# The last norm's factor scaled into the rows of w_ff1 by ScalarE, and four low parts given to VectorE

## The chip, the cores and the metric

The kernel runs on one core of one Trainium2 chip. The metric is the device time of one execution in microseconds (us). PE is TensorE's matmul row, DVE is VectorE, ACT is ScalarE, POOL is GpSimd and SP is SyncE, which issues most of the DMAs.

## What is computed

A block of a streaming encoder over 1024 tokens of 1024 features, float32. First a mixer (convolution and RWKV-7), then cross-attention with four heads into 256 memory tokens, then the MLP. What matters here is the end of the reference:

```python
x = x + cross_attention(rmsnorm(x, g_cross[l]), rmsnorm(mem, g_mem[l]), wq[l], wk[l], wv[l], wo[l])
hf = rmsnorm(x, g_ffn[l])
x = x + jnp.square(jax.nn.relu(hf @ w_ff1[l])) @ w_ff2[l]
return rmsnorm(x, g_final)

def rmsnorm(x, g):
    y = x * lax.rsqrt(jnp.mean(x * x, axis=-1, keepdims=True) + RMS_EPS)
    return y * g
```

`g_ffn` has one factor for each of the 1024 features, which are the columns of the normed tokens and the rows of `w_ff1` (1024 x 4096).

## The kernel before

All matmuls are done in three passes on pairs of a rounded high part and a low part: `split` (L70) makes the high part by a cast on ACT (L72) and the low part by a subtraction (L73), on VectorE unless another engine is given. `mm3` (L75) issues the three matmuls (L81 to L83).

The program is written as a flow of tiles, and a planner orders the instructions of each engine at build time, by a simulated timeline and by priorities (those of the order of the text, unless `at` or `shifted` moves them). On the chip each engine runs its instructions in that order. Tiles of one tag take turns in the tag's buffers. PSUM tiles of the MLP and of the attention come from a ring of eight banks (`bank`, L65): mm, pr, ep, cp, mm, pr, py, us; each user takes the next.

The attention (`attention`, L1092) goes head by head. In the last head (h == 3) the values of row block i, 128 tokens, are multiplied and added to the residual `x1[i]` (L1154), `x1[i]` is stored to `dx` (L1178), and the block is normed: `rms_scale` (L230) takes squares on ACT with their sum (L235), a sum and scale on DVE (L90) and the power -0.5 on POOL (L95); then `norm` (L242) multiplies by the token's factor and by `g_ffn` in one instruction on DVE (L246). The broadcast `g` is loaded ahead of the values of head 2 (L1172).

The up product of the MLP is a Strassen scheme with seven products. `blocks` (L1203) forms the token operands: for row blocks 0 to 3 it transposes two halves on PE (L1214) and splits them; for row blocks 4 to 7 it first takes four differences (L1238, on POOL, for block 7 on DVE), and transposes and splits five operands. Row block i follows two blocks behind the values (`feed`).

The weight operands are made by `up_operands` (L1289) for each of 16 pairs, a pair being 256 columns of `w_ff1`: two loads of 128x4x256 (L1296) into buffers that take turns (`ms`, `ms`, `w`, `w`), sums on DVE, seven splits. The first two splits of pairs 0 and 1 are given a priority of their own, inside the attention (`early`). `up` (L1325) multiplies; while it works on pair p, the operands of pair p + 1 are made, one for each product.

Of the kernel before, what the change touches and what calls it, by code (L numbers as in the profile page):

```python
# [9 lines left out]
F32 = mybir.dt.float32  # L10
F32R = mybir.dt.float32r
AF = mybir.ActivationFunctionType
ALU = mybir.AluOpType
# [4 lines left out]
P = 128  # L18
S = 1024
D = 1024  # L20
KC = D // P
# [30 lines left out]
class Trunk:  # L52
# [189 lines left out]
    def norm(self, pool, src, g, own=False):  # L242

        t, r = self.rms_scale(pool, src)
        t = src if own else t
        self.nc.vector.scalar_tensor_tensor(t, src, r, g, ALU.mult, ALU.mult)  # L246
        return t

    def features(self, t, hi, lo):
# [23 lines left out]
    def run(self):  # L273
        tc, nc, a = self.tc, self.nc, self.a
# [3 lines left out]
        def push(stack, name, bufs=1):  # L278
            cm = self.pool(name, bufs=bufs, side="right" if stack is right else None, reuse_waits="tile")
            stack.append(cm)  # L280
            return cm.__enter__()
# [5 lines left out]
        with ctx:  # L287
# [46 lines left out]
            x1 = {i: px1.tile([P, D], F32, name=f"x1_{i}") for i in (0, 4, 1, 5, 2, 6, 3, 7)}  # L334
# [23 lines left out]
            self.outs = 8  # L358
            pop(left, 2)
            pn = push(left, "pn")  # L360
            self.skip(pn, 320)
            ph1 = push(left, "ph1")
            h1 = self.norm_tiles(ph1, "h1")
            pG = push(left, "pG")
            g = self.gain(pn, "g_cross")
# [157 lines left out]
    def mixer_in(self, pc, pb, px, pl, pW, pz, hT):  # L523
# [29 lines left out]

        self.identity(pc)
        t = norm(0)
        w = conv_weights(0)
        for i in range(4):
            features(t, i)
            if i < 3:
                t = norm(i + 1)  # L560
        self.constants(pc, px)
        ts = [norm(4), norm(5)]
        conv(0, 0, *w)
        self.tap(TE[0], TE[3])
# [527 lines left out]
    def attention(self, pT, pQ, pG, pn, h1, x1, ahead, swap):  # L1092
        nc, ps = self.nc, self.ps
        scale = 256.0 ** -0.5

        def queries(h, w0=None):

            w = [w0 or self.wq_in(pG, h, 0), self.wq_in(pG, h, 1)]
            q = []
            for e in range(2):  # L1100
                for f in range(2):
                    hi, lo = (pQ.tile([P, HALF], F32R, tag="q" + t, name="q" + t, bufs=4) for t in "hl")
                    self.split(hi, lo, self.project(w[f], h1, e, P))
                    q.append((hi, lo))
            return q

        def values_in(h):
            v = []
            for m in range(2):
                st = self.pm.tile([P, D], F32, tag="ms", name="vst", bufs=2)  # L1110
                nc.sync.dma_start(st, self.dv[h, m])
                hi, lo = (pT.tile([P, D], F32R, tag=f"v{t}{m}", name="v" + t) for t in "hl")
                self.split(hi, lo, st)
                v.append((hi, lo))
            return v

        def scores(q, k, j):

            pp = self.bank(ps, "mm").rearrange("p (e m) -> p e m", m=M)
            for e in range(2):  # L1120
                ts_ = slice((2 * j + e) % 4 * P, (2 * j + e) % 4 * P + P)
                self.mm3(pp[:, e, :], [tuple(z[:, ts_] for z in q[j // 2 * 2 + f]) for f in range(2)], k)
            mx = pT.tile([P, 2], F32, tag="mx", name="mx", bufs=4)
            nc.vector.tensor_reduce(mx, pp, AX.X, ALU.max)
            nc.vector.tensor_scalar(mx, mx, -scale, None, ALU.mult)
            pe = pT.tile([P, 2, M], F32, tag="pe", name="pe", bufs=4)
            sm = pT.tile([P, 2], F32, tag="sm", name="sm", bufs=4)
            for e in range(2):
                nc.scalar.activation(
                    pe[:, e, :], pp[:, e, :], AF.Exp, bias=mx[:, e : e + 1], scale=scale, accum_out=sm[:, e : e + 1],  # L1130
                )
            nc.vector.reciprocal(sm, sm)
            for e in range(2):
                nc.vector.tensor_scalar(pe[:, e, :], pe[:, e, :], sm[:, e : e + 1], None, ALU.mult)
            return pe

        def turn(pe):
            phi, plo = (self.py_tile(F32R).rearrange("p (m t) -> p m t", m=2) for _ in range(2))
            pp = self.bank(ps, "mm")
            for m in range(2):  # L1140
                for e in range(2):
                    nc.tensor.transpose(
                        pp[:, (2 * m + e) * P : (2 * m + e + 1) * P], pe[:, e, m * P : (m + 1) * P], self.ident
                    )
            self.split(phi, plo, pp.rearrange("p (m t) -> p m t", m=2))
            return phi, plo

        def values(p, v, i):
            ts_ = slice((i % 2) * P, (i % 2) * P + P)
            for n in range(2):  # L1150
                cs = slice(n * 512, n * 512 + 512)
                pp = self.bank(ps, "mm")
                self.mm3(pp, [tuple(z[:, m, ts_] for z in p) for m in range(2)], [tuple(z[:, cs] for z in v[m]) for m in range(2)])
                nc.vector.tensor_tensor(x1[i][:, cs], pp, x1[i][:, cs], ALU.add)  # L1154

        norms = []

        def feed():
            self.blocks(*norms.pop(0), x1, B)

        q = queries(0, ahead[0])
        pe = [scores(q, ahead[1], j) for j in range(4)]
        for h in range(4):
            v = values_in(h)
            if h < 3:
                q, k = queries(h + 1), self.keys_in(pG, h + 1)
            p = [turn(t) for t in pe]
            if h < 3:
                pe = [scores(q, k, j) for j in range(4)]
            if h == 2:  # L1170
                B = swap()
                g = self.gain(pn, "g_ffn")  # L1172
            for i in range(8):
                values(p[i // 2], v, i)
                if h == 3:
                    if i > 1:
                        feed()
                    nc.sync.dma_start(self.dx[i], x1[i])  # L1178
                    norms.append((i, self.norm(pn, x1[i], g, i < 4)))
                    if i == 2:  # L1180
                        early = [self.tc.cur_priority]
        return B, feed, early
# [106 lines left out]
    def up_operands(self, p, out):  # L1289

        nc = self.nc
        st = []
        for k in range(2):
            w = next(self.wring)()
            src = self.a["w_ff1"][0, k * 512 : k * 512 + 512, p * 256 : p * 256 + 256]
            nc.sync.dma_start(w, src.rearrange("(k p) n -> p k n", p=P))  # L1296
            st.append(w)
        (a11, a21), (a12, a22) = ((w[:, :, 0:P], w[:, :, P:]) for w in st)

        def put(j, src, eng=None):  # L1300
            z = next(self.sring)().rearrange("p e (k f) -> p e k f", f=P)
            self.split(z[:, 0], z[:, 1], src, eng)
            out[j] = z[:, 0], z[:, 1]

        def temp():
            return self.temp().rearrange("p (k f) -> p k f", f=P)

        put(1, a11, nc.gpsimd if p < 2 else None)
        yield
        put(2, a12, nc.gpsimd)  # L1310
        yield
        s1 = self.both(temp(), a21, a22, ALU.add)
        s2 = self.both(temp(), s1, a11, ALU.subtract)
        put(6, s2)
        yield
        put(7, self.both(temp(), a11, a21, ALU.subtract))
        yield
        put(5, s1, nc.gpsimd)
        yield
        put(3, self.both(s2, a12, s2, ALU.subtract))  # L1320
        yield
        put(4, a22, nc.gpsimd)
        yield
# [252 lines left out]
```

## Time and profile before

| | us |
|---|---|
| median of 3 runs | 1571.23 (1570.77 to 1571.47) |
| profiled execution | 1571.13 |
| its span, from first to last instruction | 1569.4 |
| PE busy in the span | 1497.8 (95%) |
| DVE busy | 1167.2 (74%) |
| ACT busy | 665.1 (42%) |
| POOL busy | 530.9 (34%) |

Busy times are means over stages with different limits. In the rows below a time is counted from the span's start; a row's tile names are the program's (out<-in), and the brackets behind a row name the idle time ahead of it and what ended it.

### The profile page before, as it was taken

The numbers are of one execution on the slowest core, as the hardware profiler recorded it, in microseconds if no ns is written. First come the engines' busy times: TensorE is split into PE (matmuls) and PEld (weight loads), VectorE is DVE, ScalarE is ACT, GpSimd is POOL, SyncE is SP. The second block draws the span as 40 slices with busy tenths as digits, with TensorE's granted clock in tenths as the row PEclk, the third lists the DMA queues.
The fourth block names the chain that finished last, engine by engine and source line by source line (L and its number), as shares of the span: only waits on it lengthen the run. The fifth ranks groups of instructions, "written<-read, shape, count | busy, mean of one in ns | idle before, by whom it ended". The sixth has DMA issues, their size and how long they took to land. (4 is left out here: it accounts for less than half of the span.)

```text
span 1569.4 us, 22056 instructions
## 1 busy us (share of the span) xinstructions
PE 1497.8 (95%) x8114; PEld 1222.8 (78%) x8114; DVE 1167.2 (74%) x1721; ACT 665.1 (42%) x1223; POOL 530.9 (34%) x436
## 2 busy tenths in 40 slices
PE   6999887899999999999999979999999899999998
PEld 4777765668877778888888858888888788888886
DVE  5989898997889988475443787766666388578995
ACT  4522323122456653354231345555555345444454
POOL 4212337432443532431110064544444321003362
PEclk9999998897999999999999989999999999999999
DMA  7134445337334523312110132444444496563323
GB/s 236 48 128 156 124 117 171 112 117 195 108 94 123 162 98 99 101 47 81 41 41 28 52 122 86 170 152 156 156 149 157 152 382 198 178 200 87 102 80 121
DMA packets 175725, 201.14 MB, mean 128 GB/s; under 512 B 12191, under 2 KB 116951, under 8 KB 175618
## 3 DMA queue, kind: packets, MB, share of 16 engines
q1 hardware_dynamic: 168706, 187.15, 38.1%
q10 hardware_dynamic: 6912, 12.59, 2.2%
q8 instruction: 64, 1.05, 0.3%
q14 instruction: 43, 0.35, 0.1%
HBM read 139.92 MB, written 59.77 MB: 127 GB/s over the span
## 5 line engine op out<-in xcount | busy, mean ns | idle before, releaser
L629 DVE SCALAR_TENSOR_TENSOR acc<-u,cw,acc 128x1024 f32<-128x1024 f32 (+1 forms) x150 | 204.5, 1363 | 3.8
L267 POOL TENSOR_TENSOR wlo<-wst,whi 128x1024 fp32r<-128x1024 f32 (+2 forms) x34 | 86.8, 2556 | 135.9 <-ACT whi L266 135.9
L1238 POOL TENSOR_TENSOR p<-p,p 128x512 f32<-128x512 f32 x32 | 60.8, 1931 | 196.6 <-DVE p L1497 173.0
L73 DVE TENSOR_TENSOR s<-f,s 128x512 fp32r<-128x512 f32 x48 | 53.7, 1123 | 53.3 <-ACT s L72 53.3
L1343 ACT ACTIVATE y<-y 128x512 f32<-128x512 f32 x64 | 40.5, 633 | 82.0 <-DVE y L1238 74.3
L457 PE MATMUL mm<-memT,wkv 128*128 128x256 f32 x256 | 63.3, 394 | 0.0
L95 POOL TENSOR_TENSOR rsr<-rsv,mhalf 128x1 f32<-128x1 f32 x26 | 15.4, 592 | 139.7 <-DVE rsv L90 136.1
L1238 POOL TENSOR_TENSOR s<-y 128x512 f32<-128x512 f32 x32 | 41.2, 1310 | 59.8 <-ACT y L1344 59.8
L73 DVE TENSOR_TENSOR s<-y,s 128x512 fp32r<-128x512 f32 x57 | 44.9, 790 | 21.2 <-ACT s L72 21.2
L72 ACT CAST s<-y 128x512 fp32r<-128x512 f32 x57 | 35.3, 623 | 58.4 <-PE us L83 26.8
L266 ACT CAST whi<-wst 128x1024 fp32r<-128x1024 f32 (+2 forms) x34 | 35.0, 1030 | 56.8 <-issue 12.3
L893 DVE TENSOR_TENSOR fs<-xt,PL 128x4 f32<-128x4 f32 (+15 forms) x128 | 53.9, 421 | 5.9 <-ACT PL L885 3.0
L72 ACT CAST r<-y 128x512 fp32r<-128x512 f32 x55 | 33.8, 620 | 54.6 <-PE cp L83 23.2
L81 PE MATMUL mm<-hT1hi,whi 128*128 128x512 f32 (+1 forms) x120 | 50.6, 422 | 3.3 <-DVE z L513 1.8
L83 PE MATMUL mm<-hT1hi,wlo 128*128 128x512 f32 (+1 forms) x120 | 49.7, 414 | 3.8 <-POOL wlo L267 2.7
L73 DVE TENSOR_TENSOR r<-y,r 128x512 fp32r<-128x512 f32 x55 | 43.2, 791 | 13.4 <-ACT r L72 13.3
L457 PEld LDWEIGHTS mm<-memT,wkv 128*128 128x128 f32 x256 | 47.7, 195 | 6.7
L72 ACT CAST s<-w 128x512 fp32r<-128x512 f32 x69 | 42.6, 618 | 21.7 <-DMA w<-in_w_ff_dram 6.7
L1081 POOL TENSOR_TENSOR wql<-wst,wqh 128x1024 fp32r<-128x1024 f32 x8 | 20.0, 2494 | 88.0 <-ACT wqh L1080 88.0
L72 ACT CAST s<-f 128x512 fp32r<-128x512 f32 x64 | 38.0, 620 | 27.0 <-DVE f L1238 20.1
L82 PE MATMUL mm<-hT1lo,whi 128*128 128x512 f32 (+1 forms) x120 | 49.0, 408 | 0.0
L894 DVE TENSOR_REDUCE xt<-fs 128x2 f32<-128x4 f32 (+15 forms) x128 | 45.2, 353 | 3.1
(1142 smaller groups left out, 4959.5 us busy)
## 6 DMA issues: line engine op xcount, KB each, us to landing
y<-da SPq DMA_DIRECT2D x112, 256.0 KB
wst<-in_w_in_dram SPq DMA_DIRECT2D x32, 512.0 KB
w<-in_w_ff_dram SPq DMA_DIRECT2D x56, 256.0 KB
da<-y ACTq DMA_DIRECT2D x48, 256.0 KB
ms<-in_w_ff_dram SPq DMA_DIRECT2D x16, 512.0 KB
w<-in_w_ff_dram SPq DMA_DIRECT2D x16, 512.0 KB
da<-s SPq DMA_DIRECT2D x32, 256.0 KB
da<-y SPq DMA_DIRECT2D x32, 256.0 KB
```

The lines of the kernel that those rows point to most:

```text
L72: nc.scalar.copy(hi, src)
L73: (eng or nc.vector).tensor_tensor(lo, src, f32(hi), ALU.subtract)
L81: nc.tensor.matmul(ps, lh, rh, start=first and k == 0, stop=False)
L82: nc.tensor.matmul(ps, lh, rl, start=False, stop=False)
L83: nc.tensor.matmul(ps, ll, rh, start=False, stop=last and k == n - 1)
L267: nc.gpsimd.tensor_tensor(lo, st, f32(hi), ALU.subtract)
L457: nc.tensor.matmul(dst, w[:, k, :], mem[k // 4][:, k % 4, :], start=k == 0, stop=k == KC - 1)
L629: nc.vector.scalar_tensor_tensor(acc, u[:, t : t + n], self.cw[:, t * 4 + c : t * 4 + c + 1], acc, ALU.mult, ALU.add)
L893: nc.vector.tensor_tensor(tmp, x, rows, ALU.mult)
L894: nc.vector.tensor_reduce(xt[:, 0:m, 2 * k : 2 * k + 2], tmp, AX.X, ALU.add)
L1238: (eng or self.nc.vector).tensor_tensor(out, x, y, op)
L1343: nc.scalar.activation(c, c, AF.Relu)
```

## The change

The norm ahead of the MLP no longer multiplies by `g_ffn`; it multiplies by the token's factor alone, by an activation on ACT. The factors are loaded as 8 rows of 128, transposed on PE and kept as a column tile `gcol` (128x8), and the weights of each pair are multiplied by them in their buffers, with eight activations of 128x256 on ACT per pair. The low parts of the first two splits of pairs 0 and 1, before on POOL, are made on VectorE; the second split's low part of the later pairs stays on POOL.

```diff
--- before.py
+++ after.py
@@ -243,7 +243,10 @@
         t, r = self.rms_scale(pool, src)
         t = src if own else t
-        self.nc.vector.scalar_tensor_tensor(t, src, r, g, ALU.mult, ALU.mult)
+        if g is None:
+            self.nc.scalar.activation(t, src, AF.Identity, scale=r)
+        else:
+            self.nc.vector.scalar_tensor_tensor(t, src, r, g, ALU.mult, ALU.mult)
         return t
@@ -358,7 +361,8 @@
             pn = push(left, "pn")
-            self.skip(pn, 320)
+            self.skip(pn, 288)
+            self.gcol = pn.tile([P, KC], F32, name="gcol")
@@ -1169,14 +1173,18 @@
             if h == 2:
                 B = swap()
-                g = self.gain(pn, "g_ffn")
+                rows = pn.tile([P, D], F32, tag="xs", name="rows", bufs=2)[0:KC, 0:P]
+                nc.sync.dma_start(rows, self.a["g_ffn"][0].rearrange("(k p) -> k p", p=P))
+                pp = self.bank(ps, "mm")
+                nc.tensor.transpose(pp[:, 0:KC], rows, self.ident[:KC, :KC])
+                nc.scalar.copy(self.gcol, pp[:, 0:KC])
             for i in range(8):
                 values(p[i // 2], v, i)
                 if h == 3:
                     if i > 1:
                         feed()
                     nc.sync.dma_start(self.dx[i], x1[i])
-                    norms.append((i, self.norm(pn, x1[i], g, i < 4)))
+                    norms.append((i, self.norm(pn, x1[i], None, i < 4)))
@@ -1294,6 +1302,9 @@
             nc.sync.dma_start(w, src.rearrange("(k p) n -> p k n", p=P))
+            for i in range(4):
+                g = self.gcol[:, 4 * k + i : 4 * k + i + 1]
+                nc.scalar.activation(w[:, i], w[:, i], AF.Identity, scale=g)
             st.append(w)
@@ -1305,9 +1316,9 @@
-        put(1, a11, nc.gpsimd if p < 2 else None)
+        put(1, a11)
         yield
-        put(2, a12, nc.gpsimd)
+        put(2, a12, nc.gpsimd if p > 1 else None)
         yield
```

## Rows read from the trace of the kernel before

**Rows 1.** The page's first line.
```profile
span 1569.4 us, 22056 instructions
```

**Rows 2.** Busy us by stage: PE, PEld, DVE, ACT, POOL; granted clock, DMA share, GB/s.
```profile
900.00:917.00 17.00, 16.92 (x91) 13.98 (x89) 14.81 (x25) 8.81 (x17) 2.71 (x5) 1.00 0.42 165
917.00:944.00 27.00, 16.93 (x81) 12.60 (x81) 24.02 (x32) 13.47 (x25) 23.85 (x18) 0.71 0.30 103
...
958.00:1244.00 286.00, 286.00 (x1263) 236.90 (x1262) 178.82 (x225) 143.04 (x235) 137.03 (x104) 1.00 0.47 156
```

**Rows 3.** PE in order of time: start, us, line, tiles, idle before.
```profile
923.32 0.39 PE L83 MATMUL mm<-vh,y 128*128 128x512 f32 x1
...
928.94 1.11 PE L1214 MATMUL us<-ident,x 128*128 128x128 f32 x4 [2.68 <-POOL x L1238]
...
939.26 1.11 PE L1214 MATMUL mm<-ident,x 128*128 128x128 f32 x4 [0.61 <-POOL x L1238]
...
943.95 0.78 PE L81 MATMUL mm<-b1h,s 128*128 128x512 f32 x1
...
951.53 0.39 PE L81 MATMUL py<-b1h,s 128*128 128x512 f32 x1
```

**Rows 4.** POOL in order of time, 917 to 944 us.
```profile
917.79 1.28 POOL L1238 TENSOR_TENSOR x<-junk,x 128x512 f32<-128x512 f32 x1 [1.83 <-DVE rsv L90]
...
920.76 2.31 POOL L1238 TENSOR_TENSOR junk<-junk 128x512 f32<-128x512 f32 x1
...
925.50 1.72 POOL L73 TENSOR_TENSOR s<-ms,s 128x512 fp32r<-128x512 f32 x1
...
930.52 2.51 POOL L73 TENSOR_TENSOR s<-ms,s 128x512 fp32r<-128x512 f32 x2
...
936.21 1.27 POOL L1238 TENSOR_TENSOR x<-junk,x 128x512 f32<-128x512 f32 x1 [1.45 <-DVE rsv L90]
...
937.94 1.27 POOL L1238 TENSOR_TENSOR x<-junk,x 128x512 f32<-128x512 f32 x1
```

**Rows 5.** DVE: groups of 917 to 944 us, a tile's min/median/max ns, two in time.
```profile
L246 DVE SCALAR_TENSOR_TENSOR junk<-x,rsr,g 128x1024 f32<-128x1024 f32 x4 | 5.6, 1388 | 1.7 <-POOL rsr L95 1.7
L1238 DVE TENSOR_TENSOR f<-ms 128x512 f32<-128x512 f32 x2 | 3.5, 1742 | 0.0
...
L73 DVE TENSOR_TENSOR s<-w,s x52: 674/682/1780, 987.7 to 1531.1; 128x512 fp32r<-128x512 f32 x52
...
929.96 0.14 DVE L90 TENSOR_SCALAR rsv<-ssq 128x1 f32<-128x1 f32 x1
...
934.79 1.28 DVE L246 SCALAR_TENSOR_TENSOR junk<-x,rsr,g 128x1024 f32<-128x1024 f32 x1 [1.71 <-POOL rsr L95]
```

**Rows 6.** ACT in order of time, 946 to 958 us.
```profile
949.58 0.65 ACT L72 CAST s<-w 128x512 fp32r<-128x512 f32 x1
952.46 0.63 ACT L1343 ACTIVATE y<-y 128x512 f32<-128x512 f32 x1 [2.22 <-DVE y L1238]
953.00 0.60 ACT L72 CAST s<-w 128x512 fp32r<-128x512 f32 x1
```

**Rows 7.** ACT's groups: count, busy us, mean ns, idle before; then a line's min/median/max.
```profile
L235 ACT ACTIVATE junk<-x 128x1024 f32<-128x1024 f32 x16 | 17.0, 1066 | 11.2 <-DVE x L1154 11.1 <-DVE rsv L90 0.2
...
L887 ACT COPY xt<-start 128x256 f32<-128x256 f32 x8 | 3.3, 407 | 13.5 <-DVE XD L898 13.3 <-issue 0.2
...
L441 ACT ACTIVATE memT<-mm,pcol x2: 474/478/483, 158.7 to 165.0; 128x256 f32<-128x256 f32 x2
```

**Rows 8.** Loads of w_ff1 on SP's queue, a stage's traffic, a later pair's first read.
```profile
929.97 1.01 SPq L1296 DMA_DIRECT2D w<-in_w_ff_dram  x2
...
936.00:939.00 3.00, 2.20 (x8) 1.43 (x8) 1.81 (x5) 0.95 (x3) 2.79 (x3) 0.50 0.01 2
...
1070.26 6.48 SPq L1296 DMA_DIRECT2D w<-in_w_ff_dram  x2
...
1094.52 1.41 DVE L1238 TENSOR_TENSOR f<-w 128x512 f32<-128x512 f32 x1
```

## The prediction

> **What bounds the kernel now.** The profiled execution took 1571.13 us: its span of 1569.4 us [rows 1] and 1.73 us around it. It stands 0.10 us under the median of the three runs (1571.23 us), so I work on 1571.13 and a shift read from the trace carries over to the median. A change of 0.2% is 3.1 us; less than that a measurement of this kernel can hardly tell from none.
>
> I read the stage table first, because a gain in a stage where TensorE is full is worth nothing. In the stages around the change [rows 2] PE is busy 16.92 of 17.0 us before 917 us, and 286.0 of 286.0 us through the up products, 958 to 1244 us. Only 917 to 944 us is loose: PE is busy 16.93 of 27.0 us, so 10.07 us are empty, at a mean granted clock of 0.71. That stage is where the last four token blocks are normed, combined into Strassen operands and transposed, before the MLP starts. DVE is busy 24.02 and POOL 23.85 of its 27.0 us, ACT only 13.47.
>
> The second view is PE in order of time [rows 3]: the last value product starts at 923.32 us, then come single transposes, each waiting for a POOL subtraction (2.68 us at 928.94 us, 0.61 us at 939.26 us), and the first up product starts at 943.95 us. It can't come much sooner, by the code: every user of PSUM takes the next of a ring of eight banks, and product 1 of pair 0 is eighth after the third transposed block of row block 6 (the mm transposes at 939.26 us). So product 1 needs that block split, and that block needs the second subtraction of block 6, on POOL at 937.94 us [rows 4].
>
> The third view is therefore POOL [rows 4]: from 917.79 us to that subtraction it is one queue, broken by a single wait of 1.45 us at 936.21 us. Ahead of that subtraction stand nine others, powers for the norm factors, and three low parts of pair 0 (1.72 us at 925.50 us, two in 2.51 us at 930.52 us). This queue sets the end of the stage.
>
> **The change part by part.** (a) *Low parts of blocks 1 and 2 off POOL.* For pair 0 two of the three low parts leave the POOL queue: 1.72 us and half of 2.51 us, together 2.97 us off the chain. The third (block 4) stays. VectorE takes them, where the same form has a median of 0.682 us and a maximum of 1.78 us; beside a busy POOL, DVE's sums with both inputs in SBUF took 1.74 us in this stage (f<-ms, x2) [rows 5]. POOL is stretched as well: its low part took 1.72 us at 925.50 us, and 1.25 us each at 930.52 us [rows 4], a difference of 0.47 us. I charge POOL two such stretches, 0.9 us; bounds 0 (they fall into a pow or a wait) and 2.0 us (two stretches like the 2.31 us row).
>
> (b) *The norm's product moves from DVE to ACT.* Eight products of 128x1024 leave DVE; four lie in the stage, 5.6 us, mean 1.388 us [rows 5]. ACT gets them at about the price of its own 128x1024 pass with a square, 1.066 us [rows 7]. The four early ones (blocks 0 to 3) lie in 900 to 917 us, where PE is full and ACT busy 8.81 of 17 us [rows 2]: zero, covered by the value products; uncovered each would cost at most its 1.07 us. For the four late ones two effects reach POOL. First, POOL's subtraction at 920.76 us took 2.31 us while a DVE norm product ran beside it; without it I take the 1.28 us of its neighbour: 1.03 us off. Second, block 6: its sum of squares came to DVE at 929.96 us behind other DVE work, its power waited for POOL, its product started at 934.79 us, and POOL stood 1.45 us at 936.21 us for it [rows 4, 5]. With DVE relieved and POOL's queue shorter, the factor is made while POOL still works on block 5, so the 1.45 us go. Bounds: 0 if the planner keeps the power behind block 5, 1.45 us if not; I take it all, since 929.96 us lies 4.8 us ahead of the product, time that was spent in queues which get shorter. New waits: ACT's product waits for POOL's power, and the casts of finished transposes queue behind it in ACT; ACT has 13.5 us free in the stage, and at most one POOL subtraction (1.3 to 2.3 us) stands ahead of a power, which I leave in the range. The in-place products also wait on ACT for the store of the same tokens to dx; DVE had that wait before.
>
> The Trainium skill speaks against this part: "ScalarE: Activation LUTs", section "Rules for kernel authors", sends multiplications to VectorE and not to ScalarE. The trace disagrees for this form: 1.388 us on VectorE, 1.066 us for ScalarE's pass of the same size. By that rule the moved products would lengthen the stage and the sum would lose its sign.
>
> (c) *Scaling of w_ff1.* Each pair adds eight ACT instructions of 128x256. The trace has no such form from SBUF with a column as scale; the nearest are the same size copied to SBUF at 0.407 us and scaled from PSUM at 0.478 us [rows 7]. I take 0.45 us, 3.6 us per pair, 58 us in all. Where does it lie? Pair 0's low parts run only from 925.50 us [rows 4], and by the code its weights are loaded ahead of the last head's values; its 3.6 us fit into the 8.2 us that ACT idles from 900 to 917 us [rows 2]: zero, at most 3.6 us if the weights land later. From pair 2 on the weights come a whole pair ahead: issued from 1070.26 us, first read at 1094.52 us [rows 8], 18 us after the second issue, and ACT is busy 143 of 286 us; with 14 more pairs at 3.6 us it is 193 of 286. PE idles nowhere there, and operands are made a pair ahead: zero. If that cover were gone, a pair would lose at most the 3.6 us. Pair 1 is the exposed one. Its weights are issued at 929.97 us and no traffic is left after 936 us [rows 8], yet its first cast stands at 949.58 us, behind the casts of block 7, and its products follow at once: PE starts product 1 of pair 1 at 951.53 us [rows 3, 6]. If the scaling goes just ahead of each cast, 4 x 0.45 = 1.8 us come in ahead of it, ACT had 2.2 us free right after it (to 952.46 us), and the low part is 0.6 us shorter on DVE. I take 0.9 us of PE wait; bounds 0 (scaled at 936 us, in ACT's gaps) and 4.3 us (rival C).
>
> (d) *The column.* A 512 KB broadcast of g_ffn becomes a 4 KB load, one transpose, and one ACT copy, before the values of head 2, where PE is full. Four transposes of 128x128 took 1.11 us at a granted clock of 0.50 [rows 3, 8], so one costs at most 0.3 us, and less at full clock. The load waits only for a free xs buffer, as the broadcast did. I take 0.2 us; bounds 0 and, if PE reaches the transpose before the load lands, 2 us.
>
> **The sum.** Chain: -2.97 - 1.03 - 1.45 + 0.9 = -4.55 us. Exposed: +0.9 + 0.2 = +1.1 us. Together -3.45 us: 1571.13 - 3.45 = 1567.7 us. What is late next: block 7, whose four subtractions are on DVE, and ACT. ACT's load in the stage goes from 13.47 us to 13.47 + 4 x 1.07 + 12 x 0.45 = 23.2 us (pair 1, and half of pair 2) if all falls in it, in a stage of 22.5 us. So ACT can nearly take POOL's place; I don't count on more than the sum.
>
> **The rivals.** A, the forecast: 1566.0 to 1569.3 us. B, the whole gap: pair 1's scaling falls into ACT's gaps, and two more subtractions of POOL lose the stretch of 1.03 us, 2 us more, with 1 us from a start of block 4 that no longer waits for DVE (1.83 us at 917.79 us [rows 4]); 4.55 + 3 = 7.6 us off, 1563.6 us. For it: weights landed by 936 us. Against: ACT's load. C, given back at once: the planner puts pair 1's scaling behind the activation of pair 0's first output, as it already did with the second cast (953.00 us, behind 952.46 us) [rows 6]. Then PE, having ended product 2 of pair 0, waits for an add on DVE (0.7 us, as its other passes of this size), two activations, the scaling and a cast: 0.7 + 0.6 + 0.6 + 1.8 + 0.6 = 4.3 us. Sum -4.55 + 0.2 + 4.3: 1571.1 us. For it: pair 1's first cast is already just in time in the trace of before, and it gets longer while PE gets there earlier.
>
> D, slower: ACT takes POOL's place. The place is ACT's queue at 930 us: the scaling of pair 1 is put ahead of the casts of blocks 6 and 7 and waits there for the weights, issued at 929.97 us. The casts behind it stand until 936 us and another 3.6 us of scaling, so that ten casts for blocks 6 and 7, 0.6 us each, with two norm products (2.1 us) follow only from 939.6 us; the stage then ends about 947.7 us, 3.75 us later than now, and with the 0.2 us the time is 1575.1 us. It decides as soon as the queue stands more than about 4 us ahead of those casts. Beside this stands the same rule of the Trainium skill ("ScalarE: Activation LUTs", "Rules for kernel authors"). Against D: before, pair 1's casts came 13 us after the landing, so the planner expects the weights late and puts them late.
>
> **How the numbers follow.** A 0.44, B 0.13, C 0.27, D 0.16. Faster: B and all of A but 0.08 that lies above 1568.1 us: 0.49. Same: C and that part of A: 0.35. Slower: D, 0.16. The range goes from 1562.0 us (B with the bounds of (a)) to 1575.0 us, D's price, rounded; A alone is 1566.0 to 1569.3 us.
>
> **What would show it.** Right: in the new trace POOL's run from block 4's first subtraction to block 6's second lasts some 15.5 to 17 us in place of 21.4 us, with one s<-ms in it, no wait near 1.45 us, and no 2.31 us subtraction; the first up product starts near 939.4 us; PE is full to the end of the up products. Wrong (C): the same early start, and then a PE wait of 3 to 4 us on an ACT cast of w within 12 us of it. Wrong (D): ACT idle for a DMA of w between 925 and 940 us. Wrong in (c): PE waits for ACT anywhere in the up products.

## The result, and the profile after

The changed kernel takes 1581.21 us (median of 6 runs, 1577.97 to 1584.79) against 1571.28 us for the kernel before (6 runs, 1569.60 to 1571.63): a ratio of 1.0069 [1.0058, 1.0080]. It is slower by 9.9 us by the medians, 10.8 us by the ratio, and 6.2 us above the range forecast. The profiled execution is the longest of the six (1584.79 us, span 1582.8 us), so the 13.4 us between the two traces hold 3.5 us more than the medians do.

The stages first, as in [rows 2], with the same columns.

```profile
900.00:917.00 17.00, 17.00 (x87) 14.24 (x86) 10.82 (x22) 16.56 (x28) 3.31 (x6) 1.00 0.45 175
917.00:944.00 27.00, 17.66 (x102) 15.11 (x101) 22.34 (x35) 19.87 (x38) 18.07 (x16) 0.77 0.33 117
958.00:1244.00 286.00, 284.40 (x1249) 234.06 (x1248) 161.47 (x216) 172.33 (x334) 129.55 (x99) 1.00 0.43 142
```

POOL's busy time between 917 and 944 us fell from 23.85 to 18.07 us as the forecast wanted, but the first up product starts no sooner behind the last value product (20.1 us, 20.2 before). And in the up products, where PE was busy all the time before, it now idles. PE in order of time, as in [rows 3], shows each place (start, us, operation; in brackets the idle time and what ended it):

```profile
933.40 1.08 PE L1222 MATMUL cp<-ident,junk 128*128 128x128 f32 x4 [5.74 <-DVE b4l L73]
...
939.27 1.12 PE L1222 MATMUL mm<-ident,junk 128*128 128x128 f32 x4 [1.74 <-ACT junk L247]
...
944.31 0.78 PE L81 MATMUL pr<-b1h,s 128*128 128x512 f32 x1
...
954.55 0.50 PE L81 MATMUL us<-b1h,s 128*128 128x512 f32 x1 [3.55 <-ACT s L72]
...
1203.24 0.50 PE L81 MATMUL pr<-b2h,s 128*128 128x512 f32 x1 [1.60 <-ACT y L1363]
...
1268.63 0.80 PE L81 MATMUL pr<-r 128*128 128x512 f32 x1 [9.86 <-ACT r L72]
```

Three intervals between PE's rows split most of the difference: from the end of the last value product to the start of the first up product ("stage"), from there to the end of the last up product ("up"), and the idle time ahead of the first down product ("wait"). Block transposes that PE does behind the first up product (three before, 1.23 us; one after, 0.36 us) are counted with the stage. Then the three are 21.46, 305.86 and 4.22 us before, and 20.45, 314.11 and 9.86 us after. Behind the last value product stand 17 transposed blocks before and 15 after, at 0.43 us each with the clock full: 0.87 of the stage's 1.01 us only went ahead of it. So the stage by itself gained 0.14 us, and the up products with the wait behind them took 8.25 + 5.64 = 13.9 us.

A gain lies ahead of the last value product, outside the three intervals. Before, PE stood there three times, for 2.06 us together; in the changed kernel it doesn't stand there at all. The three rows of before:

```profile
917.80 0.63 PE L1214 MATMUL py<-ident,junk 128*128 128x128 f32 x4 [0.89 <-DVE rsv L90]
919.13 0.66 PE L1214 MATMUL us<-ident,x 128*128 128x128 f32 x4 [0.69 <-POOL x L1238]
920.26 0.47 PE L81 MATMUL cp<-vh,y 128*128 128x512 f32 x1 [0.48 <-DVE b2l L73]
```

With this ("ahead" in the table below) the blocks gained 2.2 us. Another 1.9 us of the 13.4 us between the traces lie ahead of the first value product, where the texts of the two kernels differ only in the size of a spare tile: it starts at 767.93 us before and at 769.81 us after, and over all 13 traces of this document, most of them of kernels with the change, at 764.1 to 769.8 us.

**The stage.** POOL's work shrank as forecast, in the rows that answer [rows 4]: the four subtractions of block 4 take 1.28 to 1.31 us each with no 2.31 us among them, one low part is left, and the last subtraction starts at 937.54 us. But its queue did not shorten as forecast. From block 4's first subtraction to the end of block 6's second (935.10 us) it takes 20.0 us, against 21.4 before and 15.5 to 17 forecast, since the one wait of 1.45 us became two: 1.26 us for block 6's norm product on ACT and 2.48 us for block 7's sum on DVE, whose power stands in the queue ahead of block 6's second subtraction.

```profile
916.40 1.31 POOL L1246 TENSOR_TENSOR x<-junk,x 128x512 f32<-128x512 f32 x1 [1.47 <-ACT junk L247]
...
919.44 1.28 POOL L1246 TENSOR_TENSOR junk<-junk 128x512 f32<-128x512 f32 x1
...
926.90 1.73 POOL L73 TENSOR_TENSOR s<-ms,s 128x512 fp32r<-128x512 f32 x1
...
930.85 1.27 POOL L1246 TENSOR_TENSOR x<-junk,x 128x512 f32<-128x512 f32 x1 [1.26 <-ACT junk L247]
934.60 0.54 POOL L95 TENSOR_TENSOR rsr<-rsv,mhalf 128x1 f32<-128x1 f32 x1 [2.48 <-DVE rsv L90]
...
937.54 1.27 POOL L1246 TENSOR_TENSOR x<-x,x 128x512 f32<-128x512 f32 x1
```

What ends the stage now is block 7. Its norm product is in ACT's queue behind the scaling of pair 2's first load, for whose landing ACT stands; DVE, which takes block 7's differences, waits 3.41 us for the product. ACT and DVE in order of time:

```profile
936.87 1.31 ACT L1307 ACTIVATE ms<-ms,gcol 128x256 f32<-128x256 f32 x3 [1.76 <-DMA ms<-in_w_ff_dram]
938.08 1.13 ACT L247 ACTIVATE junk<-x,rsr 128x1024 f32<-128x1024 f32 x1
...
939.25 1.42 DVE L1246 TENSOR_TENSOR x<-junk,x 128x512 f32<-128x512 f32 x2 [3.41 <-ACT junk L247]
```

**Pair 1.** In the rows that answer [rows 6], the second half of pair 1 is scaled behind the activation of pair 0's first output, the first cast comes behind that, and PE stands for it (the 3.55 us above).

```profile
948.81 1.71 ACT L1307 ACTIVATE w<-w,gcol 128x256 f32<-128x256 f32 x4
951.77 0.63 ACT L1354 ACTIVATE y<-y 128x512 f32<-128x512 f32 x1 [1.25 <-DVE y L1246]
952.30 1.69 ACT L1307 ACTIVATE w<-w,gcol 128x256 f32<-128x256 f32 x4
953.90 0.60 ACT L72 CAST s<-w 128x512 fp32r<-128x512 f32 x1
```

**Every later pair.** PE stays full for 250 us, but each pair leaves ACT later. The view of waits shows how long ACT stood for loads between 1000 and 1190 us (us in total, times, longest):

```profile
ACT w L1307 <- DMA w<-in_w_ff_dram: 23.9, 9, 3.7
ACT ms L1307 <- DMA ms<-in_w_ff_dram: 22.4, 8, 3.2
```

That is 46.3 us in 17 stands, none of which exists in the trace before. The chain of waits of the same stretch shows why they add up. One turn of it (start, us, what):

```profile
1091.64 1.30 POOL s L73
1092.96 3.96 DMA w<-in_w_ff_dram
...
1098.02 1.21 ACT w L1307 x3
...
1102.80 1.90 DVE f L1246 x2
1104.78 1.15 ACT s L72 x2
1106.00 1.29 POOL s L73
1107.29 4.19 issue
1111.52 1.32 POOL s L73
1112.85 4.15 DMA ms<-in_w_ff_dram
```

Block 4's low part on POOL is the last reader of a weight buffer; it frees the buffer for the load of the pair after next. That load takes 4 us to land, and ACT, whose next instruction is its scaling, stands until then. Behind ACT wait the activations, copies and casts of the present pair, and among them the cast that feeds the next pair's low part of block 4, 19.9 us later. The 4.19 us of "issue" are ACT again, which stands for the other load of the pair (its rows: 1109.22 us, behind 2.77 us of idle time). The loop closes on itself: from 1012.83 to 1217.28 us POOL's first sum of each pair comes every 20.45 us (ten turns), PE needs 19.04 us for a pair, so the copy of product 1, which frees a PSUM bank, falls behind by some 1.4 us a pair. Its lag, from the end of product 1's last matmul to the start of the copy, is 0.45 us in pair 1 (pairs count from 0), 8.67 in pair 4, 17.23 in pair 10, 20.04 in pair 12 and 20.81 in pair 13. At 20.04 us the ring of eight banks is full: product 2 of pair 13 stalls for that copy (1.60 us at 1203.24 us). The backlog is paid at the end: the first reload of the stored sums is issued at 1260.43 us instead of 1239.28 us, and ACT stands 6.04 us ahead of the first cast of a reloaded sum (the profile names a store, `da<-y`, as what ended that).

So the 13.9 us are three pieces. Up to product 1 of pair 2 the up products lose 5.5 us (44.62 us behind the first up product, 39.14 before, block transposes not counted): pair 1's wait and the half clock behind it. In pairs 13 and 14 they lose 2.7 us, 1.60 of it the stall. The wait at the end grows by 5.6 us. The last two are the loop's.

### The profile page after: what moved, and what is told of

The parts are those of the page before. It is cut to its first block, busy times and chain, and to the rows that moved or that the text cites. A ratio compares the mean times of both kernels' runs of the same rounds, so it can differ in the third digit from the quotient of the medians.

```text
span 1582.8 us, 22149 instructions
## 1 busy us (share of the span) xinstructions
PE 1501.8 (95%) x8115; PEld 1225.7 (77%) x8115; DVE 1148.2 (73%) x1717; ACT 716.0 (45%) x1360; POOL 524.0 (33%) x432
## 5 line engine op out<-in xcount | busy, mean ns | idle before, releaser
L73 DVE TENSOR_TENSOR s<-f,s 128x512 fp32r<-128x512 f32 x48 | 45.5, 952 | 93.3 <-ACT s L72 93.3
L73 DVE TENSOR_TENSOR r<-y,r 128x512 fp32r<-128x512 f32 x55 | 44.2, 809 | 13.4 <-ACT r L72 13.4
L73 DVE TENSOR_TENSOR s<-w,s 128x512 fp32r<-128x512 f32 x54 | 43.9, 814 | 12.6 <-ACT s L72 12.6
```

What stands on the lines that cost most here:

```text
L73: (eng or nc.vector).tensor_tensor(lo, src, f32(hi), ALU.subtract)
```

## The experiments

Times are medians; ratios are to the kernel before on the same chip, where its median was 1571.39 us (e1 to e4), 1569.38 us (e5, e6, f1, f2) or 1570.80 us (f4, e9, f6), so ratios compare better than times. "Ahead" is PE's idle time between 910 us and the last value product. Ahead, stage, up and wait are read from PE's rows of one execution each, as above. The kernel before and e5 have 17 transposed blocks in the stage, f4 16, the others 15; e1 and e4, which differ only from pair 1 on, differ by 0.6 us there, so less than that means nothing.

| kernel | us | ratio [95%] | ahead | stage | up | wait |
|---|---|---|---|---|---|---|
| before | 1571.28 | 1 | 2.06 | 21.46 | 305.86 | 4.22 |
| after | 1581.21 | 1.0069 [1.0058, 1.0080] | 0 | 20.45 | 314.11 | 9.86 |
| e1 no scaling | 1564.66 | 0.9959 [0.9944, 0.9973] | 0.48 | 17.19 | 304.93 | 4.22 |
| e2 scaling alone | 1584.14 | 1.0086 [1.0069, 1.0103] | 1.43 | 20.18 | 314.43 | 9.99 |
| e3 wait, no work | 1566.07 | 0.9966 [0.9954, 0.9978] | 0 | 19.02 | 304.92 | 4.21 |
| e4 work, no wait | 1564.81 | 0.9954 [0.9939, 0.9969] | 0.50 | 17.82 | 304.95 | 4.22 |
| e5 low parts alone | 1573.13 | 1.0025 [1.0015, 1.0035] | 2.41 | 22.89 | 306.34 | 4.22 |
| e6 norm on ACT alone | 1564.87 | 0.9973 [0.9958, 0.9989] | 0.57 | 18.63 | 304.96 | 4.22 |
| f1 scaling behind the copy | 1567.34 | 0.9986 [0.9973, 0.9998] | 0 | 18.06 | 306.83 | 4.59 |
| f2 f1, pair 1 on VectorE | 1565.99 | 0.9976 [0.9964, 0.9988] | 0 | 17.91 | 305.34 | 4.22 |
| f4 all scaling on VectorE | 1568.32 | 0.9988 [0.9979, 0.9997] | 0.09 | 21.84 | 304.99 | 4.22 |
| e9 pair 1 on VectorE | 1579.27 | 1.0060 [1.0045, 1.0075] | 0.20 | 20.68 | 309.61 | 9.80 |
| f6 pair 2 behind the copy | 1575.16 | 1.0027 [1.0014, 1.0039] | 0.12 | 18.06 | 310.66 | 9.96 |

### Is it the scaling, and which part of it?

**e1, the change without its scaling.**

```diff
-            for i in range(4):
-                g = self.gcol[:, 4 * k + i : 4 * k + i + 1]
-                nc.scalar.activation(w[:, i], w[:, i], AF.Identity, scale=g)
```

> The changed kernel without the scaling of the weights: the MLP is computed without g_ffn, all else of the change stays (norm's product on ACT, low parts on DVE, the column loaded but unused). Theory L (loop): in the up products a load that lands, ACT's scaling that waits for it, the first split and the rest up to the buffer's release make a loop of 20.3 us against 19.04 us of PE per pair, so outputs are read later by 1.2 us with each pair; without the scaling the loop is gone. Then product 1 is copied within 5 us of its end in every pair, the wait ahead of the first down product falls from 9.86 to about 4.2 us, the wait for pair 1 (3.55 us) goes, and the time is 1569 to 1573 us. Rival N (norm and low parts are the cause): 1579 us or more, the wait ahead of the down products stays near 9.9 us.

Measured: 6.4 us faster than before (0.41% [0.27, 0.56]), faster than theory L had it; the lag stays under 2.7 us, the wait for pair 1 is gone, and the wait at the end is 4.22 us, as L said. The loss is the scaling's; what the change does to the norm and the low parts is a gain, where 4.55 us were forecast for them.

**e2, the scaling alone:** the kernel before with the column and the three lines above.

> The kernel before with the column and the scaling of the weights added; norm and low parts as before, so g_ffn is applied twice. Theory L: the lag of the copy of product 1 grows by about 1.2 us per pair as in the changed kernel, the wait ahead of the down products is 8 to 11 us, the time 1578 to 1584 us. Rival N: 1570 to 1573 us, no growing lag.

Measured: 13.5 us slower, with the same pattern: the copy of product 1 is 4.90 us late in pair 1 and 20.62 us in pair 13, PE waits 3.55 us in pair 1 and 9.99 us at the end. The scaling alone makes the loss, without the norm's move and the low parts.

**e3, the wait without the work:** one column of the load is scaled, so ACT still stands for the landing.

```diff
-            for i in range(4):
-                g = self.gcol[:, 4 * k + i : 4 * k + i + 1]
-                nc.scalar.activation(w[:, i], w[:, i], AF.Identity, scale=g)
+            g = self.gcol[:, 4 * k : 4 * k + 1]
+            nc.scalar.activation(w[:, 0, 0:1], w[:, 0, 0:1], AF.Identity, scale=g)
```

> The changed kernel with one activation of a single column per load in place of four of 128x256: only the first of the 256 columns of one chunk per load is scaled by g_ffn. ACT still waits for each load at the same place, but has hardly any work there. Theory L: the loop is some 3 us shorter, 17 us, under PE's 19.04 us, so no growing lag, 1570 to 1574 us. Rival Q (the standing queue alone is enough): the lag grows and the time is 1577 us or more. Rival W (ACT's work is too much): 1570 to 1573 us, as theory L.

**e4, the work without the wait:** eight activations of 128x256 per pair from pair 1 on, in place of the scaling, that read the first split's high part (made just before) and write a spare tile.

```diff
+        if p > 0:
+            z = f32(out[1][0][:, 0:2])
+            for i in range(8):
+                nc.scalar.activation(self.spare, z, AF.Identity, scale=self.gcol[:, i : i + 1])
```

> The changed kernel with the scaling's eight activations of 128x256 per pair (pairs 1 to 15) kept on ACT, but reading the first split's high part, which is in SBUF already, into a spare tile: the work without the wait; g_ffn is not applied. Theory L: no loop through the load, so the lag stays bounded under some 5 us, 1571 to 1576 us. Rival W (work): ACT is as busy as in the changed kernel and the lag grows, 1578 us or more. Rival Q: 1570 to 1573 us.

Both cost next to nothing against e1, and both are faster than any theory had them, e3 by 4 us and e4 by 5 us. The times still rule out Q in e3 (1577 us or more) and W in e4 (1578 us or more); for the rest the waits and the lag decide. ACT's waits of e3 from 1000 to 1190 us, and the stretch's busy times in e4 and in the changed kernel, in that order (columns as in [rows 2]):

```profile
ACT w L1306 <- DMA w<-in_w_ff_dram: 27.6, 11, 2.9
ACT ms L1306 <- DMA ms<-in_w_ff_dram: 25.6, 9, 3.7
```

```profile
1000.00:1190.00 190.00, 190.00 (x840) 157.34 (x839) 117.19 (x150) 127.28 (x242) 89.87 (x71) 1.00 0.47 153
```

```profile
1000.00:1190.00 190.00, 190.00 (x840) 157.28 (x839) 103.28 (x142) 113.79 (x221) 83.67 (x65) 1.00 0.43 144
```

e3 stands longer for loads (53.2 us) than the changed kernel does (46.3 us), and the lag of the copy shrinks, from 3.89 us in pair 2 to 1.39 in pair 13: a turn of 18.8 us. e4 keeps ACT busier (127.28 us against 113.79), and the lag stays at 0.5 us. Neither the stands nor the work is the cause by itself; together they make one turn of the loop longer than PE's pair. That is theory L of the expectations; W, Q and N fall. L's times were too slow, since they left the other two parts 2.4 us at most, where e1 shows 6.4. And ACT's load is not the measure: with 67% of the stretch it is harmless in e4, with 60% it is fatal in the changed kernel.

**f4, the scaling on VectorE** in the same places.

```diff
-                nc.scalar.activation(w[:, i], w[:, i], AF.Identity, scale=g)
+                nc.vector.tensor_scalar(w[:, i], w[:, i], g, None, ALU.mult)
```

> The changed kernel with all scalings of w_ff1 made by VectorE instead of ScalarE, in the same places of the text. Theory L (a loop: buffer freed by a low part, load, scaling, split, low part; wait and work on one engine's queue together exceed the 19.04 us of a pair on PE): the wait for the landing moves to VectorE, one VectorE pass is shorter than 0.495 us, so the loop is some 1 us a pair shorter and the lag of product 1's copy grows by less than the 1.2 us a pair of the changed kernel, or not at all; 1566 to 1577 us, and VectorE, not ScalarE, stands for DMAs of w and ms. Rival E (only ScalarE is hurt, because its activations and copies free the PSUM banks): no lag, no wait above 5 us ahead of the first down product, 1564 to 1568 us. Rival V (VectorE, busy 63% of the up products, is the worse place): lag grows faster than 1.2 us a pair, 1583 us or more.

DVE's waits from 958 to 1240 us, and one scaling in time:

```profile
DVE w L1307 <- DMA w<-in_w_ff_dram: 12.7, 7, 2.1
DVE ms L1307 <- DMA ms<-in_w_ff_dram: 9.5, 7, 2.3
```

```profile
1080.16 1.14 DVE L1307 TENSOR_SCALAR w<-w,gcol 128x256 f32<-128x256 f32 x4 [2.12 <-DMA w<-in_w_ff_dram]
```

The loop is there too, with DVE standing in it: a turn is 19.54 us (1007.25 to 1202.61 us, ten turns), and the lag grows by 0.5 us a pair, to 11.9 us in pair 13, which isn't enough to fill the ring before the pairs end. L holds here too. E has the wait at the end (4.22 us) and nearly the time, but not the lag and the waits for loads, so it falls, and so does V. By the two ratios it is 12.7 us better than on ACT, without any cure of the cause. The stage, at 21.84 us, got worse; why stays open.

### What is each place worth?

**e9, pair 1 alone on VectorE.**

```diff
+                if p == 1:
+                    nc.vector.tensor_scalar(w[:, i], w[:, i], g, None, ALU.mult)
+                else:
+                    nc.scalar.activation(w[:, i], w[:, i], AF.Identity, scale=g)
```

> The changed kernel with only pair 1's scaling on VectorE. Theory L: PE's wait of 3.55 us in pair 1 and the half-clock stretch behind it (some 2 us) go or shrink; the lag of product 1's copy still grows by about 1.2 us a pair, now from a lower start, so the stall of 1.60 us near 1203 us may not come, and the wait ahead of the first down product stays above 5 us: 1574 to 1579 us. Rival S (the loss of the up products all descends from pair 1's late start): the lag stays below 1 us, the wait ahead of the first down product is 4.2 us, 1566 to 1570 us.

Pair 1's wait falls from 3.55 to 1.70 us (0.40 and 1.30), the half clock behind it goes (0.62 granted from 956 to 960 us in the changed kernel, 1.00 here), and up is 4.5 us shorter: 3.6 us up to product 1 of pair 2, the rest by a smaller stall of the full ring (0.70 us). The times show less of it: by the two ratios 1.4 us, with intervals that overlap. The lag grows on as before, from 1.53 us in pair 1 to 19.99 in pair 13, and the wait of 9.80 us stays. The loop needs no late start: L holds, S falls.

**f6, the scaling of pair 2 alone** queued on ACT behind the copy of pair 1's product 1.

```diff
+        return self.tc.issue_after(self.copied) if p == 2 else nullcontext()
...
+            with self.behind(p):
+                for i in range(4):
...
-        nc.scalar.copy(p1, pp)
+        self.copied = nc.scalar.copy(p1, pp).ins
```

> The changed kernel with one thing moved: the scaling of pair 2's weights is queued on ScalarE behind the copy of pair 1's product 1; later pairs as in the changed kernel. If the standing of ScalarE at 935 to 937 us for pair 2's first load, ahead of block 7's norm product, is what ate the gain of the stage before the up products, the first up product comes 17.0 to 18.5 us behind the last value product (20.1 us in the changed kernel), and the time falls by 1.5 to 3 us, if the rest stays: 1578 to 1580 us, with the lag growing by about 1.2 us a pair as before. If it was something else (the chain of block 7 on VectorE), the first up product stays 19.5 us or more behind.

The stage is 18.06 us against 20.45, so the stand for pair 2's load had eaten 2.4 us of it. Block 7's norm product now follows ACT's casts at once:

```profile
931.06 0.59 ACT L72 CAST b3h<-cp 128x512 fp32r<-128x512 f32 x1 [3.76 <-PE cp L1222]
931.70 1.15 ACT L247 ACTIVATE junk<-x,rsr 128x1024 f32<-128x1024 f32 x1
```

The time fell by more than was expected (1575.16 us, not 1578 to 1580), because the planner ordered pair 1 in another way as well: its wait there is 1.25 us. The loop is untouched: a lag of 20.52 us in pair 13, a wait of 9.96 us.

### What the other two parts are worth

**e5, the low parts alone:** the kernel before with `put(1, a11)` on VectorE for all pairs and `put(2, a12, nc.gpsimd if p > 1 else None)`.

> The kernel before with the four low parts of pairs 0 and 1 on VectorE and nothing else. By the prediction's term (a), 2.97 us leave POOL's queue and 0.9 us of stretching come back: 1569.2 us, about 2 us under the kernel before. Rival: VectorE is the engine that is full in this stage (24.0 of 27 us), so two more passes on it push the splits of the token blocks back as far as POOL moves forward: 1571 to 1573 us.

```profile
925.41 3.42 DVE L73 TENSOR_TENSOR s<-ms,s 128x512 fp32r<-128x512 f32 x2
...
932.72 0.14 DVE L90 TENSOR_SCALAR rsv<-ssq 128x1 f32<-128x1 f32 x1
...
937.17 1.27 POOL L1238 TENSOR_TENSOR x<-junk,x 128x512 f32<-128x512 f32 x1 [3.69 <-DVE rsv L90]
```

Slower by 3.9 us by the ratio; the blocks lose 1.8 us (stage and ahead), up 0.5 us, and the rest is not seen in these rows. The rival of the expectation came, not term (a). The two low parts cost DVE 1.71 us each beside a busy POOL, block 6's sum comes to DVE at 932.72 us (929.96 before [rows 5]), and POOL stands 3.69 us where it stood 1.45 [rows 4]. What left POOL's queue came back as a wait for DVE.

**e6, the norm alone:** the changed kernel without the scaling, with the low parts of the first two pairs on POOL as before.

> The changed kernel with the four low parts back on POOL and without the scaling (the MLP is computed without g_ffn): the move of the norm's product to ACT by itself. By the prediction's term (b), 1.03 + 1.45 us leave POOL's queue: 1568.8 us, and with the low parts' 2 us this makes up most of the 6.7 us that the kernel without scaling gained. Rival (the gain of the kernel without scaling is the norm's alone, by VectorE's 5.6 us): 1565 us, as without scaling.

Faster by 4.2 us, where 2.5 were expected: the stage is 21.46 - 0.87 - 18.63 = 2.0 us shorter (without the two blocks that went ahead of it), PE's waits ahead of it 1.5 us, and the up products 0.9 us; they start at full clock, 0.50 us for the first matmul, 0.78 us before [rows 3]. POOL's subtraction of 2.31 us [rows 4] takes 1.28 us here too. With the norm moved, the low parts turn into a gain: from e6 to e1 the stage goes from 18.63 to 17.19 us. That rests on one execution each; the two ratios' intervals overlap, so the times leave the rival (all of e1's gain is the norm's) open. Nor do the runs tell ACT from the lighter product: no run left the product by the token's factor alone on VectorE.

### A version that beats both

**f1:** the scaling of pair 2 and later is queued on ACT behind the copy of the product 1 of the pair before, and the first split of the next pair is asked for behind that copy.

```diff
+        return self.tc.issue_after(self.copied) if p > 1 else nullcontext()
...
+            with self.behind(p):
+                for i in range(4):
...
-            for _ in range(0 if p < 2 and j < 3 else 2 if p == 1 and j in (6, 7) else 1):
+            for _ in range(0 if (p < 2 and j < 3) or j == 1 else 2 if p == 1 and j in (6, 7) else 1):
...
-        nc.scalar.copy(p1, pp)
+        self.copied = nc.scalar.copy(p1, pp).ins
+        if p > 1:
+            next(ahead, None)
```

> The changed kernel, complete, with one thing moved: from pair 2 on the scaling of a pair's weights is queued on ACT behind the copy of the previous pair's product 1, and the first split of a pair is asked for behind that copy as well. Theory L: by then the load has landed (its issue lies 6 to 12 us ahead), ACT doesn't stand for it, the lag of the copies doesn't grow, the wait ahead of the down products is 4.2 us; pair 1 keeps most of its wait (2 to 4 us). Time 1567 to 1570 us. If the amount of ACT's work were what matters, 1578 us or more.

ACT in order of time: all eight scalings of a pair follow the copy in one run, the loads having landed by then, and ACT is idle for a load of w_ff1 for 3.3 us in the whole kernel (66.6 us in the changed one). The lag never exceeds 2.1 us. PE waits 1.3 us for pair 1, less than the 2 to 4 us expected, and 4.59 us at the end.

```profile
1094.81 0.59 ACT L1367 COPY y<-pr 128x512 f32<-128x512 f32 x1 [0.40 <-ACT y L1359]
1095.29 3.31 ACT L1311 ACTIVATE w<-w,gcol 128x256 f32<-128x256 f32 x8
1098.50 0.61 ACT L72 CAST s<-w 128x512 fp32r<-128x512 f32 x1
```

**f2:** f1 with pair 1 scaled on VectorE, as in e9.

> The kernel of the run before this one, with pair 1's weights scaled on VectorE (eight passes of 128x256 there) in place of ACT. Theory L: the wait of PE for pair 1 falls from 2 to 4 us to at most 2 us, by VectorE's faster pass (about 0.35 us each) and ACT's shorter queue; 1565 to 1568 us, faster than both kernels. If the wait for pair 1 has another cause than ACT's order, no change against the run before.

1565.99 us, 0.24% [0.12, 0.36] under the kernel before and, by the two ratios, 14.6 us under the changed one. The changed kernel, f1 and f2 do the same work on the same data; what differs is its place in the queues, and in f2 the engine for pair 1. All of PE's waits from 925 to 1300 us of f2:

```profile
PE cp L1222 <- DVE b4l L73: 5.8, 1, 5.8
PE pr L81 <- ACT r L72: 4.2, 1, 4.2
PE mm L1222 <- ACT junk L247: 1.0, 1, 1.0
PE mm L1222 <- DVE x L1246: 0.3, 1, 0.3
```

No wait is left within the up products. The 5.8 us on DVE's low part of a block, which the changed kernel has as well, are the stage's largest and are still there.

## Why the prediction was wrong

**The step that failed is (c), "from pair 2 on ... zero".** The cover was counted rightly as far as it went: a load is issued some 20 us ahead of its first reader. But a new reader was put in front. The planner's order has the scaling near the landing and not just ahead of the cast, over 20 us later (ACT scales from 1097.01 us on what it first casts at 1118.71), and on the chip ACT stands there, 2.7 us at a time, with the present pair's copies behind it. The prediction asked what ACT's work was worth in a stretch where ACT was half idle (143 of 286 us); it did not ask where in ACT's queue the new instruction stands and who is behind it. That question was put for pair 1 only, in rival D. D's mechanism is what happened, at 936.87 us for pair 2 and then in every pair, but in a stage where it had not been looked for. The bound of 3.6 us for a pair without cover was no bound on the sum either: the loop lost 1.4 us a pair, well below it, but twelve times over before the ring was full.

"Operands are made a pair ahead" held, but it covered the loss only for a time. In the trace before, the first cast of pair 8 stands 21.6 us ahead of its product 1:

```profile
1076.99 0.62 ACT L72 CAST s<-ms 128x512 fp32r<-128x512 f32 x1
...
1098.55 0.39 PE L81 MATMUL mm<-b1h,s 128*128 128x512 f32 x1
```

(A pair's own buffers are cast three times, and even pairs lie in `ms`; counted from the start, this is pair 8's first cast.) In the changed kernel this lead falls from 20.0 us in pair 2 to 4.0 us in pair 13 (1194.73 and 1198.76 us). PE waits for no operand behind pair 1; the lead and the ring of eight banks hid the loop until pair 13, so its loss shows only at the end, as a stall at 1203 us and a longer wait ahead of the down products.

**Rival C's wait came, without its early start:** 3.55 us of PE behind ACT's cast, 10.2 us after the first up product, against 4.3 us forecast; but the first up product stands at 944.31 us, not near 939.4. With the half clock behind the wait it is 5.5 us of the up products, of which e9 takes back 3.6. It is a part of the loss, not the sum.

**Terms (a) and (b) don't add, and (b) had a wait wrong.** Forecast were -2.97 + 0.9 for the low parts and -2.48 for the norm. With PE's waits ahead of the last value product counted in, the low parts alone cost 1.8 us (e5); with the norm moved they gain 1.5 us (e1 against e6). The norm alone gives 3.4 us. Both give 5.0 us, where 4.55 were forecast. That the sum fits is in part luck, since the path to it was another: of POOL's wait of 1.45 us the forecast said that it goes, and POOL stands 1.26 us for ACT and 2.48 us for DVE in its place (1.26 and 0.80 us in e1); POOL's run is 18.9 us in e1 and 20.0 in the changed kernel, not 15.5 to 17; and 1.6 of the 5.0 us are PE's waits ahead of the last value product, which the sum did not have. In the changed kernel the stand for pair 2's load takes 2.4 us of it back (f6). Another 0.9 us came in the up products of e1, e3, e4 and e6, which begin at full clock: the first matmul takes 0.78 us in the kernel before and in the changed one, and the granted clock from 944 to 948 us is 0.83 in both, against 1.00 in e1. That term was missing too; it is read from the traces and was not tested by itself.

The Trainium skill, "ScalarE: Activation LUTs", section "Rules for kernel authors", sends multiplications to VectorE. For the norm's product the move to ACT gained 4.2 us (e6): ACT takes 1.13 to 1.17 us where VectorE took 1.388 [rows 5]. That is not the same instruction, since VectorE's multiplied by the row of `g_ffn` as well, so it doesn't refute the rule. For the scaling, which is the same product on both, the runs go with it: 0.35 us on VectorE (f4, median), 0.495 us on ACT, and 1568.32 us against 1581.21. But f1, with the scaling left on ACT, takes 1567.34 us (ratio 0.9986, f4 0.9988): the place in the queue weighs as much as the engine.

**Terms that held:** the price of the norm product (1.15 us, 1.07 forecast) and of a scaling (0.495 us and 0.43 us in a run of four, 0.45 forecast), pair 0 at zero (its loads are scaled from 900 us on, with PE full), and the column: PE has no gap there.

## What to carry to other kernels

When a step is added behind a load, look up its place in the engine's queue, not the engine's busy share: an instruction that is ready early by the plan and late on the chip holds everything behind it, and if what it holds frees the next buffer, the wait comes back in every turn. Put such a step behind the last urgent instruction of the turn before; here that was worth 13 us (f1). And where PE stays full, read the lag of the instruction that frees its banks, pair by pair: a lag that grows is a loss that only shows at the end.

## What the runs showed of the hardware

A load of 512 KB lands 4.0 to 4.6 us after the release of its buffer while other transfers run (the DMA rows of the chain). DVE's subtraction with both inputs in SBUF takes 0.68 us alone and 1.71 us beside a busy POOL (e5); POOL's subtraction takes 1.28 us, and 2.31 us where VectorE's norm product ran beside it [rows 4]. The Trainium skill, "GPSIMD Engine Reference", section "1. Specifications", names contention between the two for VectorE instructions with two SBUF inputs; these rows agree, with a factor of 2.5 for VectorE.
